# Moving the long inputs' norm, the order of the FFN combinations and the first gate loads in a hybrid encoder kernel

## The chip, the cores and the metric

The kernel runs on one core of a Trainium2 chip. The metric is the device time of one execution in microseconds (us), as the median of several runs; lower is better. The engines are TensorE (PE: matmuls; PEld: its weight loads), VectorE (DVE), ScalarE (ACT), GpSimd (POOL) and SyncE (SP), which issues most of the DMA transfers.

## What is computed

The reference is a small transformer trunk of one layer. It runs twice with the same weights: on a long input of 1024 tokens and on a short one of 512. To each, 16 learned meta tokens are prepended.

```python
h = concat([meta, x])                                  # 1040 or 528 tokens, 1024 wide
n = rms_norm(h, g_mix)
qa, ka, va, qb, kb, vb = split(n @ w_in)               # 2304 columns: 18 tiles of 128
qa, ka = rotate(rms_norm(qa)), rotate(rms_norm(ka))    # group A: 8 heads, 2 key/value heads
oa = softmax(qa ka / 8) va
qb, kb = rotate(qb), rotate(kb)                        # group B: 4 heads, two softmax maps each
ob = rms_norm((softmax(..0) - lam * softmax(..1)) vb)
h = h + concat(oa, ob) @ w_out
n = rms_norm(h, g_ffn)
gate = depthwise_conv3(n @ w_gate) + conv_b            # along the tokens; 2816 = 22 tiles of 128
h = h + (gelu(gate) * (n @ w_up)) @ w_down
y = rms_norm(h, g_final)[16:]
```

All of it is float32. The kernel keeps that precision by splitting each operand into a rounded part "hi" and a remainder "lo": a product is three matmuls, hi*hi, hi*lo and lo*hi (`mm3`, lines 121 to 123). A split is a cast on ACT (line 114) and a subtraction on DVE or POOL (line 115).

## The kernel before

**Stages.** The long input is `s = 0`, the short one `s = 1`.

1. `projection` of the short input (line 197): weights come as column tiles of 128, each is loaded (`load_weight`), split and multiplied with the eight row blocks of the input, in two token chunks (256 and 272). Tiles are taken as a key or query tile of group A, then a value tile, five times; then eight key and query tiles of group B. So there are 18 tiles with two chunks each, 36 products of 24 matmuls.
2. `projection` of the long input, in three chunks (384, 384, 272), merged with the short input's `attention`.
3. The long input's `attention`, merged with everything that the short input still has to do (`mixer_out`, `conv_glu`; in the program `f1`).
4. `mixer_out_long` (line 640): the long input's product with w_out and the residual add, in three parts of its tokens (342, 344 and 340 columns; a part holds a slice of the first half of the tokens and the same slice of the second half), eight column tiles each.
5. `conv_glu_long` (line 956): gate and up products of the long input, two weight tiles at a time, as a Winograd scheme: seven half-size products in place of eight. It needs sums and differences of the four quarters of the activations (half the width by half the tokens), and of the weights' quarters.
6. The down products in the same scheme, the last norm and the output.

**The projection's passes and norm.** Before its products the projection reads the input in eight row blocks (line 228), scales and splits each (lines 234 and 235) and squares it (line 238). For the long input POOL adds the squares into `acc` (line 245). Line 249 is the first product, of key tile KA, which needs no norm yet. Then, chunk by chunk, a matmul with a matrix of 1/1024 sums `acc` over the partitions (line 255), and `rsqrt_newton` (lines 98 to 108: Ln, Exp and Square on ACT, two passes on DVE) makes `rstd`; line 257 scales it. Line 312 multiplies a product by `rstd`. The long input's products and norm share a tag of two PSUM buffers, "mm"; the short one's use "s" (three) and "t" (two).

**The combinations.** `combine` (line 654) is a generator that works on a finished part of `mixer_out_long`: its norm (a matmul, line 657, into an "s" buffer, and `rsqrt_newton`), then eight scalings of `h` (line 667), then the sums and differences for the Winograd scheme: `minus` is a subtraction on DVE (line 680), `kept` a split into one of the tiles `XS`. These tiles lie where the short input's pools were, so they can be written only when its output has left. The steps of part p's generator (`late`) are taken during part p+1, two after each tile from the third on (`ML` = 2); what is left is drained at that part's end, and the last part's steps are taken within the first gate products, three after each. In each part and tile the product is added to the residual on DVE (line 728), which frees its "s" buffer and one of two `res` buffers; POOL then issues the store of `h` (line 729).

**The first gate products.** For the first pair of gate tiles the Winograd sums of the weights are made ahead and kept in DRAM (`presplit`, `g.wg`). The products of that pair are done in two chunks of columns, 342 and 170, since the last part's 170 columns come later. `product` in `winograd` (line 916) loads its operand pair (hi and lo, 256 KB each) in each chunk anew: 7 products x 2 chunks x 2, 28 loads on SP (line 923), into `w_hi` and `w_lo` tiles with five buffers each (`HB`). `load_gate` (line 968) loads the raw gate weights and computes the gate of the meta token: 16 small products on ACT (line 977), two reductions on DVE (line 979), two matmuls (line 1004). In the before, its loads for the first pair stand behind the 18th of those loads.

**What sets the order.** Instructions are written as a program of generators; `merge` takes turns between two of them by their progress. The order in each engine's queue is then written at build time by a planner: it simulates the kernel with durations of its own and, whenever an engine is free in that simulation, gives it the ready instruction that comes first in the program. So an instruction that is late in the program can be hoisted into a hole, and a high place in the program is only a preference. On the chip the queues are fixed and strictly in order. `behind(g, ins)` (line 75) adds one rule: what is written in its block and runs on the engine of `ins` is queued after `ins`. It adds no semaphore.

Of the kernel before, what the change touches and what calls it, by code (L numbers as in the profile page):

```python
# [1 line left out]

# [10 lines left out]
F32 = mybir.dt.float32  # L13
F32R = mybir.dt.float32r
# [6 lines left out]
P = 128  # L21
# [175 lines left out]
def projection(ctx, g, s, side, tag, tag2):  # L197
# [10 lines left out]
    rstd = xp.tile([P, n], F32, name="rstd")  # L208
    products = []

    def load_tables(which):
# [9 lines left out]
    with tc.tile_pool(name=f"ps{s}", bufs=2, side=side, reuse_waits="tile") as sp:  # L221
# [25 lines left out]
        first_ps = g.psum.tile(P, cw, tag)  # L247
        with behind(g, *g.short_products):
            products.append(dense(g, first_ps, first, xhi, xlo, c0, cw))
# [7 lines left out]
        scaled = nc.vector.tensor_scalar(out=rstd, in0=rstd, scalar1=-0.5, scalar2=None, op0=ALU.mult)  # L257
        g.norm_of_short = [last, scaled.ins]
    es = ExitStack()
    bp = pool(ctx, g, f"pb{s}", 2, side)  # L260
# [107 lines left out]
    for i in range(4):  # L368
        for j in (KB + i, QB + i):
            w = load_weight(g, wp, g.w_in[j], ahead=1 + s, lo_engine=nc.gpsimd if s == 0 else None)  # L370
            for c0, cw in chunks:
# [5 lines left out]
                yield 24 * cw  # L377
    if s == 1:

        g.short_products = products[13:14]  # L380

# [258 lines left out]
def mixer_out_long(ctx, g, wp, x, begin):  # L640
# [7 lines left out]
    hp = pool(ctx, g, "fh0", 2, "right")  # L648
    cm = max(2 * w + 2 * (o == 0) for o, w in PARTS)

    def halves(a, o, w):
# [48 lines left out]
    with ExitStack() as es:  # L700
        mp = pool(es, g, "fm0", 2, "right")
        for o, w in PARTS:
# [19 lines left out]
            for j in range(KT):  # L722
                wj = load_parts(g, wp, g.wo[j]) if j in PRE else load_halves(g, wp, g.w_out[j])
                rows = g.xT[0][j * P:(j + 1) * P]
                res = loaded("res", 2, rows[:, NMETA:], rows[:, NMETA - 1:NMETA])
                ps = g.psum.tile(P, cw, "s")
                dense(g, ps, wj, xhi, xlo, 0, cw, range(KT - 1, -1, -1))
                nc.vector.tensor_tensor(out=h[:, j], in0=ps, in1=res, op=ALU.add)
                nc.gpsimd.dma_start(out=halves(g.h[j], o, w),
                                    in_=h[:, j, :2 * w].rearrange("p (x t) -> p x t", x=2))  # L730
                if o == PARTS[-1][0] and j >= KT - 2:

                    sums.append(mp.tile([P, cm], F32, name="sq_p", tag="m", bufs=MB)[:, :cw])
                    nc.scalar.activation(sums[-1], h[:, j], AF.Square)
                else:
                    add_square(g, mp, acc, h, j, 0, cw, nc.gpsimd, 1)
                yield 24 * cw
                if late and j >= ML:
                    for _ in range(2):
                        next(late, None)  # L740
            if late:
# [155 lines left out]

def winograd(g, wp, up, x, raw, c0, cw, pre=None):

# [16 lines left out]
    def product(a, b, place):  # L916
        if pre is None:
            a = split_half(g, wp, a)
        else:
            i, half = place  # L920
            a = [wp.tile([P, H], F32R, name=nm, tag=nm, bufs=HB) for nm in ("w_hi", "w_lo")]
            for part, tl in enumerate(a):
                g.loads.append(nc.sync.dma_start(out=tl.bitcast(F32),
                                                 in_=pre[i, part, :, half * H:(half + 1) * H]).ins)
        ps = g.psum.tile(P, cw, "mm")
        for i in range(HT):
            mm3(g, ps, *block(a, i), b[0][:, i, c0:c0 + cw], b[1][:, i, c0:c0 + cw], i == 0, i == HT - 1)
        return ps
# [27 lines left out]
def conv_glu_long(ctx, g, wp, x, late, es_x, es_h):  # L956
# [8 lines left out]
    first = PARTS[-1][0]  # L965
    g.loads = []

    def load_gate(f0):


        with behind(g, *g.loads[17:18] if f0 == 0 else g.loads[-1:] if f0 == 2 else []):
            raw = [load_whole(wp, g, g.w_gate[f0 + i]) for i in range(2)]
# [10 lines left out]
    for f0 in range(0, NFF, 2):  # L983
# [4 lines left out]
        for c0, cw in ((0, first), (first, H - first)) if f0 == 0 else ((0, H),):  # L988
            for i, half, ps, rest in winograd(g, wp, up, x, raw if f0 else None, c0, cw, None if f0 else g.wg):
                t0 = 1 + half * H + c0  # L990
                nc.vector.tensor_tensor(out=gate[:, i, t0:t0 + cw], in0=ps, in1=rest, op=ALU.add)
                for _ in range(3):
                    next(late, None)
            if f0 + c0 == 0:
                drain(late)
        if f0 == 0:
            raw, first_sums = load_gate(f0)
        if not ap:
            es_h.close()
            ap = pool(es, g, "fa0", 1, "left")  # L1000
        act = ap.tile([P, 2, N], F32, name="act", tag="act", bufs=2)
        for i in range(2):
            ps = g.psum.tile(P, 2, "mm")
# [13 lines left out]
        if f0 + 2 == NFF:  # L1017
            with tc.issue_after(gelu.ins):
                nc.scalar.preload_act_table_set(EXP_LN)
        raw = [load_whole(up, g, g.w_up[f0 + i], "w_f2") for i in range(2)]  # L1020
        for i, half, ps, rest in winograd(g, wp, up, x, raw, 0, H):
            a = act[:, i, half * H:(half + 1) * H]
# [224 lines left out]
def drain(gen):  # L1247
    for _ in gen:
        pass


LAG = 5
NPRE = 4
# [17 lines left out]
def trunk_kernel(ctx, tc, g):  # L1271
# [69 lines left out]
    g.splits = []  # L1341
    with ExitStack() as es:
        drain(projection(es, g, 1, "right", "s", "t"))
    g.splits = None
    with ExitStack() as es0:
        p0 = projection(es0, g, 0, "left", "mm", "mm")
        with ExitStack() as es1:
            merge(attention(es1, g, 1, "right"), R1[0], p0, R1[1])
        drain(p0)
# [92 lines left out]
```

## Time and profile before

| | us |
|---|---|
| three runs | 2128.84, 2129.21, 2135.24 |
| their median | 2129.21 |
| the profiled execution | 2138.1 |
| its span, first to last instruction | 2136.3 |
| mean granted TensorE clock in it | 0.982 |
| PE busy | 2051.1 |
| DVE busy | 1724.1 |
| ACT busy | 1156.8 |
| POOL busy | 582.7 |

The profile is of one execution. Times in its rows count from the span's start. A row of the timeline is start, duration, engine, line, instruction, output<-inputs, shapes, how many in a row, and in brackets how long the engine sat idle before it and what ended that wait. PE's busy time is that of pipelined matmuls, whose shown durations overlap; the granted clock is 1.00 at full speed and 0.50 at half. In this execution the short products run to 152, the long input's projection beside the short one's attention from there to about 510, the three parts of `mixer_out_long` from 1320 to 1449, the gate and up products from there to 1900.

### The profile page before, as it was taken

Reading aid. Unit: us, or ns where it says so; the run is one execution under the profiler, and the core shown is the slowest. Engines: PE = TensorE matmul, PEld = TensorE weight load, DVE = VectorE, ACT = ScalarE, POOL = GpSimd, SP = SyncE. Lnnn points to the kernel's source line nnn. Section 1 sums busy time; section 2 is a strip of 40 time slices with the busy share of each in tenths; the row PEclk is TensorE's granted clock in tenths of the full one; section 3 lists DMA queues with packets and bytes.
Section 4 is the critical chain, followed back from the end, with each engine's and each line's share of the span. In section 5 each row is a group of like instructions: output and inputs, shape, how many; then the busy total and the mean of one; then the engine's idle time right before and its main releaser. Section 6 shows DMA issues by size and latency. Waiting matters only on the chain.

```text
span 2136.3 us, 35264 instructions
## 1 busy us (share of the span) xinstructions
PE 2051.1 (96%) x12302; PEld 1833.1 (86%) x12302; DVE 1724.1 (81%) x3786; ACT 1156.8 (54%) x2253; POOL 582.7 (27%) x534
## 2 busy tenths in 40 slices
PE   6999999999999999999999999979999999999998
PEld 6988888997887999899989999978888777778877
DVE  6878889767879788888988885578878878869886
ACT  6635566544657556666666765345444444435454
POOL 4653233553112000000000000542444444330112
PEclk8999999999999999999999999998999999999999
DMA  7564335456621322223352224986232232247443
GB/s 252 178 198 133 118 110 170 153 182 226 206 84 55 105 75 70 70 85 114 103 188 77 93 88 145 300 256 229 101 109 89 97 115 84 94 166 258 119 126 126
DMA packets 164897, 296.30 MB, mean 139 GB/s; under 512 B 21456, under 2 KB 82672, under 8 KB 164208
## 3 DMA queue, kind: packets, MB, share of 16 engines
q1 hardware_dynamic: 162416, 287.76, 41.6%
q0 software_dynamic: 2304, 6.29, 0.8%
q8 instruction: 97, 1.59, 0.3%
q14 instruction: 80, 0.66, 0.1%
HBM read 211.13 MB, written 82.85 MB: 138 GB/s over the span
## 4 chain that ended last, share of the span: by engine, by line
PE 76%; DVE 12%; DMA 4%; ACT 3%; issue 3%; POOL 1%; SPq 1%; DVEq 0%; ACTq 0%; POOLq 0%
PE ps_mm L121 17%; PE ps_mm L123 17%; PE ps_mm L122 17%; PE ps_t L456 5%; PE ps_s L431 3%; PE ps_s L432 3%; PE ps_s L121 2%; PE ps_s L122 2%; PE ps_s L123 2%; PE ps_o L471 2%; PE ps_o L470 2%; DVE p L433 1%; DVE w_lo L115 1%; DMA m<-oT 1%; DVE acc L979 1%
## 5 line engine op out<-in xcount | busy, mean ns | idle before, releaser
L121 PE MATMUL ps_mm<-xhi,w_hi 128*128 128x258 f32 (+3 forms) x1264 | 383.4, 304 | 12.0 <-ACT xhi L114 3.7
L122 PE MATMUL ps_mm<-xlo,w_hi 128*128 128x258 f32 (+3 forms) x1264 | 379.0, 300 | 0.3 <-POOL xlo L115 0.3
L123 PE MATMUL ps_mm<-xhi,w_lo 128*128 128x258 f32 (+3 forms) x1264 | 377.2, 299 | 0.3 <-DVE w_lo L115 0.3
L433 DVE TENSOR_SCALAR_CACHE_REDUCE p<-ps_s 114x344 f32<-114x344 f32 (+4 forms) x562 | 257.6, 488 | 30.2 <-PE ps_s L432 19.1
L114 ACT CAST pt_hi<-ps_t 128x512 fp32r<-128x512 f32 (+6 forms) x360 | 169.3, 483 | 181.0 <-PE ps_t L456 155.2
L121 PEld LDWEIGHTS ps_mm<-xhi,w_hi 128*128 128x128 f32 x1264 | 240.0, 190 | 17.5 <-ACT xhi L114 5.4
L438 ACT ACTIVATE p<-p,nm 114x1040 f32<-114x1040 f32 (+5 forms) x212 | 214.8, 1013 | 72.8 <-DVE nm L436 71.8
L115 DVE TENSOR_TENSOR w_lo<-w_f,w_hi 128x1024 fp32r<-128x1024 f32 (+1 forms) x182 | 192.8, 1067 | 66.2 <-ACT w_hi L114 65.6
L122 PEld LDWEIGHTS ps_mm<-xlo,w_hi 128*128 128x128 f32 x1264 | 240.3, 190 | 1.9 <-POOL xlo L115 0.7
L123 PEld LDWEIGHTS ps_mm<-xhi,w_lo 128*128 128x128 f32 x1264 | 240.0, 190 | 1.2 <-DVE w_lo L115 0.5
L114 ACT CAST w_hi<-w_f 128x1024 fp32r<-128x1024 f32 (+1 forms) x199 | 167.6, 856 | 84.9 <-PE ps_mm L122 57.5
L115 DVE TENSOR_TENSOR pt_lo<-ps_t,pt_hi 128x512 fp32r<-128x512 f32 (+4 forms) x312 | 171.7, 561 | 43.7 <-ACT pt_hi L114 42.3
L115 POOL TENSOR_TENSOR a_lo<-gate,a_hi 128x256 fp32r<-128x256 f32 x44 | 43.3, 985 | 545.3 <-ACT a_hi L114 525.9
L431 PE MATMUL ps_s<-k,q 128*114 128x348 f32 (+4 forms) x552 | 183.6, 338 | 3.4 <-DVE p L433 3.2
L456 PE MATMUL ps_t<-ident,p 128*128 128x128 f32 (+7 forms) x1188 | 183.0, 270 | 1.0 <-DVE nm L436 0.5
L432 PE MATMUL ps_s<-k,q 128*114 128x348 f32 (+4 forms) x552 | 171.1, 315 | 0.0
L121 PE MATMUL ps_s<-xhi,w_hi 128*128 128x256 f32 (+4 forms) x480 | 148.7, 313 | 20.4 <-ACT xhi L234 8.2
L456 PEld LDWEIGHTS ps_t<-ident,p 128*128 128x128 f32 (+7 forms) x1188 | 140.4, 136 | 29.6 <-issue 6.8
L123 PE MATMUL ps_s<-xhi,w_lo 128*128 128x256 f32 (+4 forms) x480 | 147.4, 307 | 1.4 <-DMA w_lo<-wo 1.4
L122 PE MATMUL ps_s<-xlo,w_hi 128*128 128x256 f32 (+4 forms) x480 | 148.6, 310 | 0.0
L121 PE MATMUL ps_mm<-t_hi,w_hi 128*128 128x512 f32 (+2 forms) x368 | 144.6, 393 | 1.2 <-DVE v L934 1.2
L123 PE MATMUL ps_mm<-t_hi,w_lo 128*128 128x512 f32 (+2 forms) x368 | 144.4, 392 | 0.1
(275 smaller groups left out, 5309.4 us busy)
## 6 DMA issues: line engine op xcount, KB each, us to landing
w_f<-w_gate SPq DMA_DIRECT2D x46, 512.0 KB, 3.5
w_f<-w_up SPq DMA_DIRECT2D x44, 512.0 KB, 3.4
w_f<-w_in SPq DMA_DIRECT2D x36, 512.0 KB, 3.9
a_f<-act SPq DMA_DIRECT2D x62, 256.0 KB, 2.7
w_f<-w_down SPq DMA_DIRECT2D x22, 512.0 KB, 3.3
act<-a_t SPq DMA_DIRECT2D x44, 256.0 KB, 2.1
a<-w_down SPq DMA_DIRECT2D x40, 256.0 KB, 5.4
w_hi<-wo SPq DMA_DIRECT2D x36, 256.0 KB, 5.1
```

Of the source, the lines that this page charges most:

```text
L114: return (nc.scalar.copy(hi, src).ins, (lo_engine or nc.vector).tensor_tensor(out=lo, in0=src, in1=hi.bitcast(F32), op=ALU.subtract).ins)
L115: (lo_engine or nc.vector).tensor_tensor(out=lo, in0=src, in1=hi.bitcast(F32), op=ALU.subtract).ins)
L121: nc.tensor.matmul(ps, lhsT=whi, rhs=xhi, start=start, stop=False)
L122: nc.tensor.matmul(ps, lhsT=whi, rhs=xlo, start=False, stop=False)
L123: return nc.tensor.matmul(ps, lhsT=wlo, rhs=xhi, start=False, stop=stop).ins
L431: nc.tensor.matmul(ps, lhsT=q[0], rhs=k[:, c0:c0 + cw], start=True, stop=False)
L432: nc.tensor.matmul(ps, lhsT=q[1], rhs=k[:, c0:c0 + cw], start=False, stop=True)
L433: nc.vector.tensor_scalar(out=p[:, c0:c0 + cw], in0=ps, scalar1=HD ** -0.5, scalar2=-3.0e38, op0=ALU.mult, op1=ALU.max, accum_out=mx[:, i: ...
L438: g.last_exp = nc.scalar.activation(p, p, AF.Exp, bias=nm, accum_out=l).ins
L456: nc.tensor.transpose(tps[:, c:c + M], p[:, k0:k0 + kw], g.ident[:M, :M])
L470: nc.tensor.matmul(o, lhsT=v[:, i, :], rhs=hi, start=i == 0, stop=False)
L471: nc.tensor.matmul(o, lhsT=v[:, i, :], rhs=lo, start=False, stop=False)
```

## The change

It has four parts.

- **Projection.** `projection` of the long input yields once when its passes, first product and norm are written. The short projection's generator is run for 24 chunks (`TN`), that is 12 of its 18 tiles; then the long one's first stretch is written; then the short one's last six tiles. Everything else of the long projection still follows after these. The first long product stays behind the 14th short one.
- **Combinations.** The two steps after each tile stand behind that tile's residual add on DVE.
- **First gate operands.** An operand pair is loaded in the first chunk and kept for the second. Five pairs stay in the five buffers of `w_hi` and `w_lo`; the other two go to a third tile `h` from the pool of `mixer_out_long` (two buffers), which is free when part 1's combinations are done. The raw gate weights' loads stand behind the last of the 14 loads that are left.
- **Meta token's sums.** For the first pair, the first two up products come ahead of the two matmuls of line 1004. For every pair the loads of the up weights are written before the gate's activation.

```diff
 def projection(ctx, g, s, side, tag, tag2):
+    if s == 1:
+        g.short_products = products
...
-        with behind(g, *g.short_products):
+        with behind(g, *(g.short_products[13:14] if s == 0 else [])):
             products.append(dense(g, first_ps, first, xhi, xlo, c0, cw))
...
         g.norm_of_short = [last, scaled.ins]
+    if s == 0:
+        yield 0
...
-    if s == 1:
-        g.short_products = products[13:14]

 def mixer_out_long(ctx, g, wp, x, begin):
     hp = pool(ctx, g, "fh0", 2, "right")
+    g.spare_h = lambda: hp.tile([P, KT, cm], F32, name="h", tag="h")
...
-                nc.vector.tensor_tensor(out=h[:, j], in0=ps, in1=res, op=ALU.add)
+                added = nc.vector.tensor_tensor(out=h[:, j], in0=ps, in1=res, op=ALU.add).ins
...
                 if late and j >= ML:
-                    for _ in range(2):
-                        next(late, None)
+                    with behind(g, added):
+                        for _ in range(2):
+                            next(late, None)

 def winograd(g, wp, up, x, raw, c0, cw, pre=None, kept=None, more=None):
...
+        elif place in kept:
+            a = kept[place]
         else:
             i, half = place
-            a = [wp.tile([P, H], F32R, name=nm, tag=nm, bufs=HB) for nm in ("w_hi", "w_lo")]
+            if len(kept) < HB:
+                a = [wp.tile([P, H], F32R, name=nm, tag=nm, bufs=HB) for nm in ("w_hi", "w_lo")]
+            else:
+                a = [more[:, (2 * (len(kept) - HB) + part) * H:][:, :H].bitcast(F32R) for part in range(2)]
+            kept[place] = a
             for part, tl in enumerate(a):
                 g.loads.append(nc.sync.dma_start(...))

 def conv_glu_long(ctx, g, wp, x, late, es_x, es_h):
+    more = g.spare_h().rearrange("p k c -> p (k c)")
     def load_gate(f0):
-        with behind(g, *g.loads[17:18] if f0 == 0 else g.loads[-1:] if f0 == 2 else []):
+        with behind(g, *g.loads[-1:] if f0 == 0 else g.loads[-1:] if f0 == 2 else []):
...
         act = ap.tile([P, 2, N], F32, name="act", tag="act", bufs=2)
+        raw = [load_whole(up, g, g.w_up[f0 + i], "w_f2") for i in range(2)]
+        products = winograd(g, wp, up, x, raw, 0, H)
+        ahead = [next(products)] if f0 == 0 else []
         for i in range(2):
             ps = g.psum.tile(P, 2, "mm")
             nc.tensor.matmul(ps, lhsT=first_sums[i], rhs=g.ones_d[:, 0:2], start=True, stop=True)
...
-        raw = [load_whole(up, g, g.w_up[f0 + i], "w_f2") for i in range(2)]
-        for i, half, ps, rest in winograd(g, wp, up, x, raw, 0, H):
+        for i, half, ps, rest in chain(ahead, products):

+TN = 24
 def trunk_kernel(ctx, tc, g):
...
-    with ExitStack() as es:
-        drain(projection(es, g, 1, "right", "s", "t"))
-    g.splits = None
     with ExitStack() as es0:
         p0 = projection(es0, g, 0, "left", "mm", "mm")
+        with ExitStack() as es:
+            p1 = projection(es, g, 1, "right", "s", "t")
+            for _ in range(TN):
+                next(p1)
+            next(p0)
+            drain(p1)
+        g.splits = None
         with ExitStack() as es1:
             merge(attention(es1, g, 1, "right"), R1[0], p0, R1[1])
```

More of the change, by code (lines that the diff above doesn't have):

```diff
@@ L1 @@
 from contextlib import ExitStack, nullcontext
+from itertools import chain
 import numpy as np
@@ L895, in presplit, with winograd @@
     yield 0
-def winograd(g, wp, up, x, raw, c0, cw, pre=None):
+def winograd(g, wp, up, x, raw, c0, cw, pre=None, kept=None, more=None):
     nc = g.nc
@@ L965, in conv_glu_long @@
     first = PARTS[-1][0]
-    g.loads = []
+    g.loads, kept = [], {}
+    more = g.spare_h().rearrange("p k c -> p (k c)")
     def load_gate(f0):
-        with behind(g, *g.loads[17:18] if f0 == 0 else g.loads[-1:] if f0 == 2 else []):
+        with behind(g, *g.loads[-1:] if f0 == 0 else g.loads[-1:] if f0 == 2 else []):
             raw = [load_whole(wp, g, g.w_gate[f0 + i]) for i in range(2)]
@@ L988, in conv_glu_long @@
         for c0, cw in ((0, first), (first, H - first)) if f0 == 0 else ((0, H),):
-            for i, half, ps, rest in winograd(g, wp, up, x, raw if f0 else None, c0, cw, None if f0 else g.wg):
+            for i, half, ps, rest in winograd(g, wp, up, x, raw if f0 else None, c0, cw, None if f0 else g.wg, kept, more):
                 t0 = 1 + half * H + c0
```

## The prediction

> **What bounds the kernel now.** I read the page first, for the busiest engine.
>
> ```profile
> span 2136.3 us, 35264 instructions
> ...
> PE 2051.1 (96%) x12302; PEld 1833.1 (86%) x12302; DVE 1724.1 (81%) x3786; ACT 1156.8 (54%) x2253; POOL 582.7 (27%) x534
> ```
>
> TensorE (PE) sets the time: 96% busy. An order that changes no amount of work can only win back PE's idle time, 2136.3 - 2051.1 = 85.2 us, and the time in which PE runs at half clock. So I asked next for PE's waits, longest first (who waited for whom: us in total, times, longest). The longest of all, and a short one, belong to lines that the change touches; two more stand below, under part A:
>
> ```profile
> PE ps_s L657 <- DVE h L728: 8.5, 1, 8.5
> ...
> PE ps_mm L121 <- DVE v L934: 1.2, 1, 1.2
> ```
>
> Then the busy table of the stretches around these waits. Its columns are the stretch, its length, each engine's busy time (and instructions), the granted clock, the DMA share and GB/s.
>
> ```profile
> 152.00:156.40 4.40, 1.70 (x7) 0.68 (x6) 2.87 (x5) 2.00 (x4) 2.24 (x3) 1.00 0.62 193
> 156.40:163.20 6.80, 4.74 (x15) 4.75 (x16) 2.20 (x4) 1.87 (x4) 0.55 (x3) 0.50 0.90 277
> ...
> 1390.00:1402.00 12.00, 11.58 (x70) 10.95 (x70) 7.57 (x13) 3.72 (x9) 7.39 (x10) 1.00 0.95 305
> 1402.00:1416.00 14.00, 11.23 (x64) 9.71 (x62) 8.05 (x16) 6.75 (x14) 7.95 (x13) 1.00 0.83 276
> 1416.00:1424.50 8.50, 0.04 (x1) 0.07 (x1) 8.26 (x12) 3.19 (x5) 0.00 (x0) 0.70 0.67 215
> 1424.50:1429.60 5.10, 5.10 (x16) 4.63 (x17) 2.70 (x4) 2.66 (x6) 3.96 (x5) 0.50 0.66 192
> 1429.60:1449.00 19.40, 18.39 (x115) 17.56 (x113) 18.28 (x27) 8.56 (x14) 6.64 (x8) 1.00 0.86 254
> 1449.00:1462.60 13.60, 13.60 (x86) 13.51 (x85) 11.47 (x17) 5.16 (x9) 4.28 (x2) 1.00 0.96 332
> 1462.60:1465.20 2.60, 2.60 (x26) 2.60 (x24) 2.60 (x5) 0.61 (x2) 0.00 (x0) 1.00 0.96 336
> 1465.20:1467.20 2.00, 0.70 (x6) 0.42 (x4) 2.00 (x4) 1.56 (x4) 0.00 (x0) 0.99 1.05 399
> 1467.20:1477.50 10.30, 10.30 (x48) 10.30 (x49) 8.03 (x13) 6.64 (x21) 0.00 (x0) 0.50 0.84 289
> 1477.50:1484.20 6.70, 6.70 (x20) 5.44 (x19) 6.60 (x10) 4.97 (x14) 1.28 (x1) 0.50 0.00 1
> ...
> 1500.00:1900.00 400.00, 396.70 (x1709) 318.08 (x1708) 330.40 (x377) 178.45 (x355) 179.98 (x118) 1.00 0.28 98
> ```
>
> Three places are to be seen: after the short projection (152 to 163), before the long inputs' second norm (1402 to 1430) and in the first gate products (1465 to 1484). Each has an idle PE and, after it, half clock. From 1500 to 1900 PE is idle for 3.3 of 400 us; nothing is to be had there.
>
> **Part A, the long inputs' passes and norm.** The moved step issues 9 loads on SP, the split of one weight, 16 ACT passes, 8 DVE passes, 21 POOL adds, 24 matmuls, and then three norm chunks: a matmul, three ACT and two DVE instructions each, one scaling on DVE. In program order they now pass the last six short tiles, that is six weight loads with their splits, twelve products, and the rotations' stores on SP. But the order is a planner's, and it had already hoisted all but the last two norm chunks:
>
> ```profile
> L245 POOL TENSOR_TENSOR acc<-acc,x x21: 941/1177/2012, 36.7 to 79.1; 128x384 f32<-128x384 f32 x14, 128x272 f32<-128x272 f32 x7
> ```
>
> The adds, which need the loads and the passes, were over by 81 us. So this part of the move costs and brings nothing: the cover is that PE has short products from 108 to 152. What really moves, in the timeline:
>
> ```profile
> 83.88 0.81 PE L255 MATMUL ps_mm<-acc,ones_d 128*128 128x384 f32 x2
> ...
> 152.19 0.81 PE L255 MATMUL ps_mm<-acc,ones_d 128*128 128x384 f32 x2
> ...
> 155.52 0.70 PE L255 MATMUL ps_mm<-acc,ones_d 128*128 128x272 f32 x2 [2.52 <-DVE rstd L106]
> ...
> 158.46 0.69 PE L121 MATMUL ps_mm<-xhi,w_hi 128*128 128x384 f32 x1 [2.24 <-DVE rstd L106]
> 158.91 0.70 DVE L257 TENSOR_SCALAR rstd<-rstd 128x1040 f32<-128x1040 f32 x1
> ...
> 159.95 0.18 POOL L504 CAST halo<-q 128x2 fp32r<-128x2 f32 x1 [4.02 <-DMA q<-qk]
> ```
>
> One of the two "mm" buffers holds the first product, so the norm chunks take turns in the other: matmul, Ln, Exp, Square, DVE, next matmul. The first went at 84, the other two only when the short tiles were out. In front of the last six tiles they lie beside those tiles' matmuls, and PE goes from the short products straight to the long ones. Won: 2.52 + 2.24, and half of the 4.74 us that PE worked at clock 0.50, 2.4: in all 7.2. What is late next is the attention's operand q, at 159.95 as before; until then PE has the second and third key products (158.46 less 152.19 is 6.3 us that they come earlier). Between nothing (the waits move along) and 7.2, I take 7.2, since the three rows carry it directly.
>
> Here the Trainium skill speaks against me. Its page "TensorE: Matmul & The Clock Gate", section "What's actually happening", has the clock drop after an idle window of about 3.4 us. No single wait between 152 and 163 is that long, nor is PE's pause at 1465, yet the stretches behind both show 0.50, so the trace disagrees and decides. By the page the 2.4 would not be this step's to win, and the sum would be 4.8 for A.
>
> **Part B, combinations behind adds.** The edges bind only DVE: in part p+1, the combination steps of part p stand behind the add of tile 2, 3 and so on. The chain of waits (start, us, what) and DVE's timeline (start, us taken, instruction) show what stands there now:
>
> ```profile
> 1388.92 1.45 DVE h L667 x3
> 1390.37 0.44 DVE h L728
> 1390.83 3.38 DMA res<-xT
> 1394.30 0.53 DVE h L728
> 1394.84 5.96 DMA res<-xT
> 1400.87 7.51 DMA m<-oT
> ```
> ```profile
> 1386.75 3.63 DVE L667 SCALAR_TENSOR_TENSOR h<-h,gain,rstd 128x340 f32<-128x340 f32 x6
> 1390.30 0.50 DVE L728 TENSOR_TENSOR h<-ps_s,res 128x344 f32<-128x344 f32 x1
> ...
> 1414.75 1.63 DVE L115 TENSOR_TENSOR x_lo<-h,x_hi 128x680 fp32r<-128x680 f32 x2
> ...
> 1423.80 0.93 DVE L728 TENSOR_TENSOR h<-ps_s,res 128x340 f32<-128x340 f32 x2
> ```
>
> Six L667, 3.63 us, stood ahead of the add at 1390.30; with edges two may stand there, 1.2 us. So the add, the residual loads behind it (two buffers, each free only after an add) and all later SP loads come 2.4 us earlier: queued behind the add are also POOL's store of h and the sum of squares. The 8.5 us wait is another matter: the adds at 1423.80 belong to part 2, the burst from 1414.75 to part 0, which stays ahead of part 2 in program order. No edge touches it; it moves only as far as its start does, and it starts once the short inputs' output lets go of its memory. Bounds: above, PE's losses (8.5 idle, 14.00 - 11.23 = 2.8, half of 5.10 = 2.5), 13.8, but DVE must do the same work before the gate and is idle from 1402 on for 14.00 - 8.05 + 8.50 - 8.26 + 5.10 - 2.70 + 19.40 - 18.28 + 13.60 - 11.47 = 11.8 us; below, 0, since the DMA share of 0.95 may eat an earlier issue. I take 3, near the 2.4 that the row shows. What the edges hold back in part 2 (its last step, three passes of 0.8 as in the burst) falls into a wait that DVE has anyway, for the third norm:
>
> ```profile
> 1451.03 0.57 DVE L106 SCALAR_TENSOR_TENSOR rstd<-ps_s,eps,rstd 128x340 f32<-128x340 f32 x1 [3.07 <-ACT rstd L105]
> ```
>
> Without that cover it would cost 2.5. The edges are an order in DVE's own queue and add no semaphore; behind a held combination wait ACT's casts of it and, last, the gate's products.
>
> **Part C, gate operands once, sums later.** The fourteen loads of this row (from the DMA issues of 1438 to 1470; count, KB each, median us to landing) and their fourteen w_lo twins become seven each; that is 14 x 256 KB less on DMA engines that are full here (share 0.96 to 1.05). Behind it stand a row of the chain of waits and one of DVE's timeline:
>
> ```profile
> w_hi<-wg SPq DMA_DIRECT2D x14, 256.0 KB, 5.1
> ```
> ```profile
> 1459.26 7.87 DMA w_lo<-wg
> ```
> ```profile
> 1466.09 0.50 DVE L934 TENSOR_TENSOR v<-ps_mm,u 128x342 f32<-128x342 f32 x1
> ```
>
> The load issued at 1459.26 landed at 1467.13, where PE's third 170-wide matmul waited for it. But PE's 1.2 us wait before that is for L934, which frees PSUM at 1466.59: that wait takes the place of the loads'. Won: 1467.13 - 1466.59 = 0.5. Two operand pairs now go to a spare h tile, so SP waits for part 1's last combination; w_up, w_gate and w_down loads are queued behind. The pair is needed by the sixth of seven products, about 1449 + 5/7 of 13.6 = 1458.7; issued by 1451, when DVE's last held pass is through, and 5.1 under way, it lands at 1456. Cost taken: 0 (0 to 2, if it is a long one such as the 7.87). The sums' products and reductions only move behind two 512-wide products and lie under them: 0. The up weights' loads of later groups come earlier on SP: 0, PE has no gap there.
>
> The half clock after 1467.2 costs (49 weight loads in 10.30, against 24 in 2.60: 10.30 - 49 x 0.108 = 5.0) plus half of 6.70, 8.3 in all. I credit none of it, because it may not be in the timed runs: the profiled execution took 2138.1, 8.9 above their median of 2129.21.
>
> **Sum.** 7.2 + 3 + 0.5 = 10.7. Against the profiled execution's 2138.1 that gives 2127.4; against the median, **2118.5**. The forecast's own range is 2112 to 2123.
>
> **Rivals.**
>
> *All three places open* (chance 0.18). The short inputs' output ends earlier, the burst spreads over DVE's idle 11.8, the clock stays up: 7.2 + 8 to 11.8 + 0.5, and up to 8.3: 2113 down to 2101. For it: DVE idles 5.9 us just before the burst. Against: DVE is full from 1462.6 to 1467.2.
>
> *The clock after the norm isn't bought back* (0.08): the two waits go and PE still runs at 0.50 for a stretch there, since DMA-bound starts of the attention leave it thin. 2118.5 + 2.4 = 2120.9. By the clock gate page of the Trainium skill this is the case to expect.
>
> *The norm's waits move* (0.18). PE takes its queue in order; if the planner puts the second and third L255 too close together among the short tiles, the 2.52 and 2.24 appear there. Then only 3.5 are left: 2125.7, no change.
>
> *DVE becomes the bound at the gate: slower* (0.16). With fewer loads ahead of them the raw gate weights land earlier, and their sums move up into the stretch where DVE is full:
>
> ```profile
> 1469.75 1.91 DVE L979 TENSOR_REDUCE acc<-prod 128x128 f32<-128x1024 f32 x1
> ```
>
> ```profile
> L977 ACT ACTIVATE prod<-w_f,x 128x128 f32<-128x128 f32 x16 | 4.9, 387 | 2.2 <-DVE acc L979 2.2
> ```
>
> Two reductions ahead of L934 hold PSUM 3.8 us longer; one weight's eight products on ACT, in front of the t_hi cast that DVE waits for, 8 x 0.387 = 3.1 more; and so long a wait makes the half clock certain, 8.3 that the timed runs may not pay now. With B lost in the same queue: 2129.2 - 7.2 - 0.5 + 15.2 = 2136.7. It decides once a reduction stands ahead of the second L934. Against it: the sums are later in program order, so they come first only where the planner sees DVE idle.
>
> **How the numbers follow.** The forecast has 0.40. A run of this kernel can be told from no change at about 0.3%, 6.4 us, so faster means below 2122.8 and slower above 2135.6. Faster: 0.38 of the forecast, 0.06 of the clock case, 0.18 of the first rival: 0.62. Same: 0.04 of these two, 0.15 of the moved waits, 0.04 of the last: 0.23. Slower: 0.15. The range goes from within the first rival, 2103, to the last one's price, 2137.
>
> **What would show it.** A: L255's three chunks before the last short product, no L106 wait of PE, granted clock 1.00 at 156. B: at most two L667 between the adds of part 1, a first add of part 2 still behind x_lo/t_lo passes, PE's wait at L657 near 6 us. C: 14 loads of wg, a wait for L934 of about a microsecond left. I am wrong if L657's wait is gone or grown, or if L979 stands ahead of L934.

## The result, and the profile after

The changed kernel is slower: 2144.36 us (median of four runs) against 2130.77, a ratio of 1.0063 (95% interval 1.0049 to 1.0077), that is 13 us (10 to 16). I had forecast 2118.5 and a range up to 2137. The profiled execution after took 2142.1 (span 2140.3). That it lies only 4.0 us above the one before is due to the one before: of 35 further runs of the kernel before only one, at 2137.66, came near its 2138.1, and their median is 2129.27.

Line numbers after are up to 14 higher: 116 is the lo pass (115 before), 434 a score matmul (431), 661 the norm of a part (657), 671 the scaling (667), 732 the residual add (728), 946 and 1005 the gate's additions (934, 991), 993 the meta sums' reduction (979). In the experiments they lie a few lines off these; the names of the tiles tell which is meant.

The page after, and TensorE's waits of that kernel:

```profile
span 2140.3 us, 35241 instructions
...
PE 2049.3 (96%) x12302; PEld 1832.2 (86%) x12302; DVE 1737.8 (81%) x3786; ACT 1156.5 (54%) x2253; POOL 580.8 (27%) x534
```
```profile
PE ps_s L661 <- DVE h L732: 8.5, 1, 8.5
...
PE ps_s L434 <- DVE p L436: 5.6, 5, 2.2
...
PE ps_mm L123 <- DVE t_lo L116: 3.9, 2, 3.6
```

No wait for the norm is left. Idle PE is 2140.3 - 2049.3 = 91.0 us, 5.8 more than before. Where it is, the busy table after shows (columns as in the prediction):

```profile
152.00:156.40 4.40, 4.39 (x24) 3.78 (x23) 1.21 (x3) 0.76 (x2) 1.54 (x2) 1.00 0.72 212
156.40:163.20 6.80, 5.43 (x36) 4.72 (x35) 3.00 (x9) 3.53 (x7) 1.21 (x4) 1.00 0.91 281
...
200.00:300.00 100.00, 96.11 (x595) 86.69 (x593) 82.88 (x245) 58.76 (x131) 28.42 (x28) 0.97 0.39 118
300.00:400.00 100.00, 92.71 (x577) 85.47 (x576) 89.84 (x284) 60.66 (x158) 35.55 (x25) 0.91 0.47 145
...
1471.00:1488.10 17.10, 13.72 (x54) 12.85 (x55) 10.28 (x20) 8.57 (x17) 3.86 (x3) 0.50 0.21 72
```

and the same two stretches before:

```profile
200.00:300.00 100.00, 97.09 (x616) 87.62 (x617) 84.48 (x250) 59.97 (x135) 30.77 (x29) 1.00 0.41 125
300.00:400.00 100.00, 94.63 (x621) 86.70 (x621) 86.82 (x293) 64.05 (x167) 35.21 (x25) 1.00 0.49 151
```

At 152 to 163 all is as forecast: PE busy 9.82 of 11.20 us in place of 6.44, at clock 1.00. Between 200 and 400, which my sum left alone, PE is busy 2.9 us less and the granted clock falls to 0.97 and 0.91. And at the gate stands the rival that I had given 0.16. VectorE's timeline, then TensorE's waits there:

```profile
1464.12 0.51 DVE L1005 TENSOR_TENSOR gate<-ps_mm,u 128x342 f32<-128x342 f32 x1
1464.55 1.98 DVE L993 TENSOR_REDUCE acc<-prod 128x128 f32<-128x1024 f32 x1
1466.44 1.64 DVE L116 TENSOR_TENSOR t_lo<-h,t_hi 128x680 fp32r<-128x680 f32 x2
1467.99 0.51 DVE L946 TENSOR_TENSOR u<-ps_mm,u 128x342 f32<-128x342 f32 x1
...
1469.61 1.90 DVE L993 TENSOR_REDUCE acc<-prod 128x128 f32<-128x1024 f32 x1
...
1473.46 0.86 DVE L116 TENSOR_TENSOR t_lo<-h,t_hi 128x680 fp32r<-128x680 f32 x1
```
```profile
1470.12 0.46 PE L122 MATMUL ps_mm<-t_hi,w_hi 128*128 128x170 f32 x2 [1.31 <-ACT t_hi L115]
...
1474.38 0.51 PE L123 MATMUL ps_mm<-t_lo,w_hi 128*128 128x170 f32 x1 [3.58 <-DVE t_lo L116]
```

One reduction stands ahead of the first 342-wide L946, the other ahead of the last t_lo passes, and PE waits for t_hi and t_lo. Half clock follows for 17.1 us, as long as it does in the trace of before (10.30 and 6.70 in the prediction's table).

### The profile page after: what moved, and what is told of

Same layout as the page of the kernel before. It is cut to its first block, busy times and chain, and to the rows that moved or that the text cites. A ratio compares the mean times of both kernels' runs of the same rounds, so it can differ in the third digit from the quotient of the medians.

```text
span 2140.3 us, 35241 instructions
## 1 busy us (share of the span) xinstructions
PE 2049.3 (96%) x12302; PEld 1832.2 (86%) x12302; DVE 1737.8 (81%) x3786; ACT 1156.5 (54%) x2253; POOL 580.8 (27%) x534
## 4 chain that ended last, share of the span: by engine, by line
PE 75%; DVE 13%; DMA 4%; issue 3%; ACT 3%; POOL 1%; SPq 1%; DVEq 0%; ACTq 0%; POOLq 0%
PE ps_mm L122 17%; PE ps_mm L124 17%; PE ps_mm L123 17%; PE ps_t L459 5%; PE ps_s L434 3%; PE ps_s L435 3%; PE ps_s L123 2%; PE ps_s L122 2%; PE ps_s L124 2%; DVE w_lo L116 2%; PE ps_o L474 2%; PE ps_o L473 1%; DVE p L436 1%; DVE acc L993 1%; DMA m<-oT 1%
## 5 line engine op out<-in xcount | busy, mean ns | idle before, releaser
L436 DVE TENSOR_SCALAR_CACHE_REDUCE p<-ps_s 114x344 f32<-114x344 f32 (+4 forms) x562 | 257.8, 488 | 28.4 <-PE ps_s L435 15.2
L123 PE MATMUL ps_mm<-t_lo,w_hi 128*128 128x512 f32 (+2 forms) x360 | 141.6, 393 | 3.9 <-DVE t_lo L116 3.9
```

The source lines that it names most:

```text
L123: nc.tensor.matmul(ps, lhsT=whi, rhs=xlo, start=False, stop=False)
L436: nc.vector.tensor_scalar(out=p[:, c0:c0 + cw], in0=ps, scalar1=HD ** -0.5, scalar2=-3.0e38, op0=ALU.mult, op1=ALU.max, accum_out=mx[:, i: ...
```

## The experiments

In each, the time is compared with runs of the kernel before that stand beside it; a ratio of 1.001 is 2.1 us. The ratio is an estimate from all of these runs and not the quotient of the two medians; `a_r08` and `a_held_fill` have five runs, the others eleven or twelve.

### Each part alone

`a_alone` has the projection's part of the diff, `b_alone` the two hunks of edges, `cd_alone` the gate's two parts, `d_alone` only the later sums:

```diff
+        raw = [load_whole(up, g, g.w_up[f0 + i], "w_f2") for i in range(2)]
+        products = winograd(g, wp, up, x, raw, 0, H)
+        ahead = [next(products)] if f0 == 0 else []
         for i in range(2):
             ps = g.psum.tile(P, 2, "mm")
...
-        for i, half, ps, rest in winograd(g, wp, up, x, raw, 0, H):
+        for i, half, ps, rest in chain(ahead, products):
```

> Only the long inputs' passes and norm stand in front of the last six short tiles; the combinations, the gate operands and the meta sums are as before. Theory 1 (the projection and the attention of the short inputs lose more than the early norm wins): 4 to 8 us slower than before, ahead of it by about 7 us at 160 us and behind it by 2 to 5 us at 540 us. Theory 2 (what the changed kernel loses sits at the gate, and the trace of before was an unlucky one there): 3 to 7 us faster than before, and the 2.5 and 2.2 us waits for the norm are gone without new ones.

> Only the edges: the steps of a combination stand behind the add of the tile before them. My prediction: 3 us faster (0 to 5), at most two passes of h<-h,gain,rstd between two adds of part 1, and PE's longest wait (for the first add of part 2) unchanged but for its start, 8 us. Rival (the edges push the last passes of part 1 and with them those of part 2 towards the gate's products): 2 to 5 us slower, lost between 1440 and 1480 us.

> Only the gate: operands of the first gate products loaded once, meta sums' products behind the first up product; edges and norm as before. Theory 1 (the raw gate weights now land earlier, and two reductions of 1.9 us stand on VectorE in front of the t_lo passes that TensorE waits for): 3 to 5 us slower, all of it between 1465 and 1480 us, with a wait of 3 us or more for t_lo. Theory 2 (the gate is neutral, as predicted; the wait for t_lo comes from the edges): within 1.5 us of before.

> Only the order at the end of the gate: the meta sums' products (and what needs them) stand behind the first up product; the gate operands are loaded twice as before, no edges, norm as before. Theory 1 (the loads are what moves the reductions up; the later sums by themselves only take away TensorE's wait for the second sum, 3.1 us in the kernel with the edges alone): 1 to 4 us faster than before, no wait of TensorE for acc. Theory 2 (the later sums cost, since up weights then pass the gate's): 2 us or more slower.

| | median | before | ratio (95%) | us |
|---|---|---|---|---|
| a_alone | 2134.92 | 2129.27 | 1.0031 (1.0020 to 1.0042) | +6.6 |
| b_alone | 2130.26 | 2129.27 | 1.0008 (0.9994 to 1.0022) | +1.7 |
| cd_alone | 2135.46 | 2129.27 | 1.0037 (1.0025 to 1.0048) | +7.9 |
| d_alone | 2129.62 | 2128.51 | 1.0001 (0.9992 to 1.0011) | +0.2 |

(The last column is the ratio less one, times 2129.) The three parts add up to 16.2, near the 13.4 of the whole. Two lose; the edges and the later sums do nothing that can be measured. The gate operands were not run without the later sums, so that the 7.9 is theirs follows from `cd_alone` against `d_alone`. Theory 1 holds for the norm. For the gate it holds in kind only: 7.9 us where 3 to 5 were expected, and TensorE waits more for t_hi (3.93) than for t_lo (1.15). For the later sums neither expectation came.

My 3 us for the edges were not there. In `b_alone` the add of part 1 came 1.5 us after the first scaling (1377.40 and 1375.88), where it had come 3.6 us after it (1390.30 and 1386.75): 2.0 us earlier, for the 2.4 of the forecast. But the DMA share is 0.98 there, and in the 12 us from 1380 PE, waiting for weights, is busy for 10.46, no more than the 11.58 of before. The busy table of `b_alone`:

```profile
1365.00:1380.00 15.00, 15.00 (x98) 14.57 (x96) 13.40 (x21) 5.81 (x14) 12.59 (x19) 1.00 0.98 315
1380.00:1392.00 12.00, 10.46 (x64) 9.71 (x63) 7.62 (x13) 3.75 (x10) 6.54 (x8) 1.00 0.84 286
```

The kernel `b_alone` runs the stages up to 1330 exactly as before, so it serves as a second trace of before there. The busy table of `b_alone`, then of `a_alone`:

```profile
140.00:160.00 20.00, 15.23 (x107) 14.22 (x106) 11.86 (x22) 6.88 (x14) 9.18 (x14) 0.92 0.54 176
160.00:200.00 40.00, 36.81 (x215) 33.78 (x215) 32.94 (x109) 19.97 (x47) 13.50 (x19) 0.87 0.39 130
...
200.00:500.00 300.00, 292.27 (x1907) 274.48 (x1906) 234.25 (x699) 165.96 (x403) 120.67 (x102) 0.99 0.46 147
```
```profile
140.00:160.00 20.00, 19.99 (x149) 19.38 (x148) 10.29 (x21) 5.47 (x11) 10.04 (x13) 1.00 0.50 163
160.00:200.00 40.00, 35.55 (x216) 32.37 (x215) 36.03 (x110) 20.27 (x46) 16.38 (x21) 0.96 0.50 169
...
200.00:500.00 300.00, 285.56 (x1848) 268.28 (x1847) 239.75 (x693) 163.45 (x397) 117.94 (x100) 0.98 0.43 140
```

To 200 the early norm wins 3.5 us of idle PE (60 - 52.04 against 60 - 55.54) and up to 5.2 us of clock (0.08 of 20 and 0.09 of 40). From 200 to 500 it loses 6.7 us of busy PE, and some 3 us by the clock (0.98 of 300 us in place of 0.99). The gain is real, and more than all of it goes in a stage that the edit does not touch.

These two sums leave 1 us of loss, and the runs show 6.6. Counting the columns that TensorE has worked off (128x384 is 384), `a_alone` is 8.1 us ahead of `b_alone` at 200, 3.1 behind at 500, 5.4 at 545 and 8.9 at 1300. The part behind 500 can't be put down to the edit: the kernel before, in the order of `b_alone` to there, is 8.9 us behind `b_alone` at 1300 too.

### Where the norm stands, and the mix behind it

`a_alone` with one constant changed:

```diff
-TN = 24
+TN = 30                                   # a_tn30
...
-R1, R2, R3 = (1.0, 0.9), (1.0, 0.4), (1.0, 20.0)
+R1, R2, R3 = (1.0, 0.8), (1.0, 0.4), (1.0, 20.0)   # a_r08
```

> The early norm alone, in front of the last three short tiles and not the last six. Theory 1 (the loss after 200 us comes from the first long products, which start 6 us earlier against the attention, wherever the norm stands): 4 to 9 us slower than before, as with six tiles, with the same waits between 300 and 400 us. Theory 2 (each place of the norm gives another plan of the attention's stage, better or worse by chance): another set of waits there, and a time that differs from that with six tiles by more than 3 us.

> The early norm alone (in front of the last six short tiles), and the long projection's share beside the short attention lowered from 0.9 to 0.8, so that the attention runs ahead again. Theory 1 (the early long products put the projection ahead of the attention and so work on VectorE together at 300 to 400 us): the waits between 300 and 400 us fall from 9.2 to 5 us or less, and the kernel is 4 us or more faster than with the early norm alone. Theory 2 (any other mix loses against the one of before): as slow as the early norm alone or slower, 6 us or more above before.

`a_tn30` 2134.76 against 2128.51, ratio 1.0028 (1.0018 to 1.0038); `a_r08` 2138.01, 1.0040 (1.0027 to 1.0052). So the place of the norm does not matter (theory 1), and a smaller share of the long projection does not help: my first guess at the mechanism, too much projection over the whole stage, falls. In both, the third chunk of long products still runs ahead of the attention's first scores (from 158 and 156 us).

### That one chunk held back

```diff
     def product(w, c0, cw):
         ps = g.psum.tile(P, cw, tag)
-        products.append(dense(g, ps, w, xhi, xlo, c0, cw))
+        with behind(g, *(g.scores[5:6] if s == 0 and len(products) == 2 else [])):
+            products.append(dense(g, ps, w, xhi, xlo, c0, cw))
```

(`g.scores` collects the second matmul of each score product. The chunk is the third of the key tile KA, and it is queued behind the sixth score product.)

> The early norm alone, with one order added on TensorE: the long projection's third chunk product stands behind the first six score matmuls of the short attention, as it does in the kernel before (with the early norm it ran ahead of them). Theory 1 (that one chunk of lead is what makes another order of the 200 to 500 us, with its waits and half clock): the waits between 200 and 500 us fall back from 14.4 us to 8, and the kernel is 1 to 5 us faster than before (TensorE then waits 2 to 4 us for q at 157 us). Theory 2 (the early norm itself costs there, by other passes on VectorE): still 4 us or more slower than before.

2123.64 against 2128.31: ratio 0.9980 (0.9968 to 0.9991), 4 us faster than before and 11 faster than `a_alone`. TensorE now waits for q, and the later waits are those of before again. The timeline and the waits (160 to 400 us) of `a_held`, then the waits of `b_alone` and of `a_alone`, and a row of the busy table of `a_held`:

```profile
159.11 1.00 PE L434 MATMUL ps_s<-k,q 128*128 128x264 f32 x3 [3.58 <-DMA q<-qk]
```
```profile
PE ps_mm L121 <- DVE hn L106: 2.1, 1, 2.1
PE ps_o L474 <- DVE pt_lo L115: 1.4, 2, 0.8
PE ps_s L434 <- DVE p L436: 1.3, 3, 0.5
```
```profile
PE ps_mm L339 <- DVE t L333: 3.3, 2, 2.3
PE ps_mm L121 <- DVE hn L106: 2.1, 1, 2.1
PE ps_o L471 <- DVE pt_lo L115: 1.5, 2, 0.9
PE ps_s L431 <- DVE p L433: 1.2, 3, 0.5
```
```profile
PE ps_s L433 <- DVE p L435: 5.2, 4, 2.2
PE ps_mm L121 <- DVE t L317: 2.2, 1, 2.2
```
```profile
200.00:500.00 300.00, 291.05 (x1900) 273.37 (x1899) 232.77 (x695) 162.50 (x395) 123.29 (x107) 0.99 0.47 150
```

TensorE's idle time from 200 to 500 is 9.0 us, 7.7 in `b_alone` and 14.4 in `a_alone`. An idle of 3.6 us in front of the attention is cheaper than the 24 matmuls that filled it: with them ahead, the planner wrote another order for all that follows. The traces show that order: of the 754 groups of like instructions that VectorE runs in `b_alone` from 162 to 500, 725 stand in the same sequence in `a_held` and 502 in `a_alone` (TensorE: 1593 and 1282 of 1621).

### The meta sums held back

```diff
-            for k in range(KT):
-                nc.scalar.activation(prod[:, k], ...)
-            nc.vector.tensor_reduce(out=acc, ...)
+            with behind(g, *g.adds[3:4] if f0 == 0 else []):
+                for k in range(KT):
+                    nc.scalar.activation(prod[:, k], ...)
+                nc.vector.tensor_reduce(out=acc, ...)
```

(`g.adds` collects the gate's additions; the fourth is the last 342 wide.) `sums_held` has it on the changed kernel, `cd_held` on `cd_alone`.

> The changed kernel, but the first pair's meta sums (ScalarE's products and VectorE's reductions) are held behind the last of the four 342-wide gate additions. Theory 1 (the two reductions of 1.9 us in front of t_lo cost the wait of 3.6 us and make the stretch at half clock there): 4 to 8 us faster than the changed kernel, so 6 to 10 us slower than before, no wait for t_lo over 1 us. Theory 2 (VectorE is full there whatever the order; its burst of 680-wide passes is what is late): within 1.5 us of the changed kernel, 12 to 15 us slower than before.

> The gate part alone (operands once, later sums), without edges and early norm, with the first pair's sums held behind the last of the four 342-wide gate additions. Theory 1 (the 7.9 us that the gate part lost are the reductions and ScalarE's products ahead of the t passes): 6 to 9 us faster than the gate part alone, so from 2 us faster to 2 us slower than before; no wait for t_hi or t_lo over 2 us. Theory 2 (they are the fewer, earlier loads themselves): still 5 us or more slower than before.

`sums_held`: 2134.98 against 2129.27, 1.0030 (1.0018 to 1.0043), so 7 us of the 13 come back. `cd_held`: 2128.36 against 2128.51, 0.9995 (0.9986 to 1.0005), all of the 7.9. Theory 1 holds in both, but for its sign that no wait for t_lo over 1 us is left in `sums_held` (1.7). The rule binds only what runs on the engine of the addition, VectorE, so it holds the two reductions; ScalarE's products come later only where they wait for a reduction (the first eight still run at 1452.20 in `cd_held`). What had put the sums there is the loads, which `cd_held` issues nearly as early (1445.40) without the loss. The SP queue's issues of the first two pairs of raw gate weights, before and in `cd_alone`:

```profile
1457.77 0.90 SPq L150 DMA_DIRECT2D w_f<-w_gate  x2
...
1469.34 5.16 SPq L150 DMA_DIRECT2D w_f<-w_gate  x2
```
```profile
1442.87 1.44 SPq L151 DMA_DIRECT2D w_f<-w_gate  x2
...
1452.20 4.99 SPq L151 DMA_DIRECT2D w_f<-w_gate  x2
```

Of the 14.9 and 17.1 us between these times, 7.6 are that `cd_alone` came there earlier as a whole (its last norm stands at 1440.92, before at 1448.53); the rest is the gate part's, which has 14 loads in front of them in place of 18 and more. ScalarE's timeline in `cd_alone`, then TensorE's waits in `cd_alone` and in `cd_held`:

```profile
1461.47 2.45 ACT L988 ACTIVATE prod<-w_f,x 128x128 f32<-128x128 f32 x8 [3.98 <-DVE acc L990]
1463.82 1.41 ACT L115 CAST t_hi<-h 128x680 fp32r<-128x680 f32 x2
```

```profile
1464.62 0.51 PE L122 MATMUL ps_mm<-t_hi,w_hi 128*128 128x170 f32 x1 [3.93 <-ACT t_hi L115]
1466.27 0.51 PE L123 MATMUL ps_mm<-t_lo,w_hi 128*128 128x170 f32 x1 [1.15 <-DVE t_lo L116]
```
```profile
1462.69 0.34 PE L122 MATMUL ps_mm<-t_hi,w_hi 128*128 128x170 f32 x1 [0.28 <-ACT t_hi L115]
1464.30 0.35 PE L123 MATMUL ps_mm<-t_lo,w_hi 128*128 128x170 f32 x1 [1.26 <-DVE t_lo L116]
```

The eight products at 1461.47 are already the second pair's. They had waited for the second reduction to free the one `prod` buffer, and the casts of t_hi stand behind them.

### The price of the half clock

(`g.last_dense` is the last product of `mixer_out_long` so far; nothing reads `fill`.)

```diff
+        if o == PARTS[1][0]:
+            fill = g.psum.tile(P, P, "o")
+            with behind(g, g.last_dense):
+                for _ in range(34):
+                    nc.tensor.matmul(fill, lhsT=g.ones_d, rhs=g.ones_d, start=True, stop=True)
         ps = g.psum.tile(P, cw, "s")
```

> The kernel before with 34 matmuls of ones by ones (128 wide, 7.5 us at full clock, nothing reads them) in the 8.5 us wait ahead of the norm in the middle of the long mixer output; nothing else differs. Theory 1 (a wait makes half clock when it leaves TensorE idle for 2 us or more of one window of 3.41 us, and that half clock costs as much as a short wait): no half clock after the wait, where all traces so far have 10.2 us of it, so 5 us faster. Theory 2 (the half clock there comes from something else, such as the DMA-fed products behind the wait): within 1.5 us of before.

> The gate part alone with its sums held, and the same 34 matmuls in the wait. If the two are independent: 5 to 6 us faster than before (1 us of the held sums, 5 us of the clock).

`fill` 2125.52 against 2128.31, 0.9990 (0.9977 to 1.0002); `cd_held_fill` 2128.09, 0.9990 (0.9976 to 1.0005). Neither can be told from no change, and neither reaches the 5 us that I had expected; in `cd_held_fill` the two medians differ by 0.2 us only. TensorE's timeline of `fill`, two stretches behind the wait in `fill`, and the stretch before that is like the first:

```profile
1406.76 7.75 PE L659 MATMUL ps_o<-ones_d 128*128 128x128 f32 x68
1415.41 0.82 PE L662 MATMUL ps_s<-acc,ones_d 128*128 128x344 f32 x2 [0.91 <-DVE h L733]
...
1438.24 0.84 PE L662 MATMUL ps_s<-sq_p,ones_d 128*128 128x340 f32 x2 [1.97 <-ACT sq_p L739]
```
```profile
1414.50:1425.00 10.50, 9.60 (x61) 9.42 (x61) 8.19 (x16) 4.59 (x9) 4.19 (x6) 1.00 0.74 205
...
1436.00:1444.00 8.00, 6.03 (x26) 5.57 (x26) 4.82 (x10) 2.40 (x6) 0.68 (x1) 0.79 1.00 357
```
```profile
1424.50:1435.00 10.50, 10.50 (x51) 10.03 (x52) 8.06 (x15) 4.75 (x9) 4.59 (x6) 0.76 0.71 193
```

Each of the 34 runs in two passes, hence 68. The clock stays at 1.00, where it was 0.76 on the mean, as theory 1 says. Of the 5 us that I had put on it, 1.0 goes into the next wait: for the squares of the last part TensorE waited 1.01 us before and waits 1.97 now. Behind that wait comes half clock that was not there before (0.79 over 8 us, about 1.7). By these rows some 2.4 would be left, near the 2 of the runs.

### Put together

`all_held_fill` is the changed kernel without the edges, with both orders and the 34 matmuls; `mended` the whole changed kernel with both orders; `a_held_fill` is `a_held` with the 34 matmuls.

> Early norm with the third chunk held, gate part with its sums held, and the 34 matmuls in the wait; no edges. If theory 1 holds for each: 7 to 11 us faster than before, the fastest kernel of all. If the early norm costs by itself: slower than the same kernel without it.

> The whole changed kernel, edges included, with the two orders put back: the long projection's third chunk behind the first six score matmuls, and the first pair's meta sums behind the last 342-wide gate addition. Theory 1 (these two orders are all that the change lost): 13.4 us of loss less what the two give back alone (6.6 + 4.7 = 11.3 for the chunk, 7.9 + 1.1 = 9 for the sums) is 7 us faster than before; anything from 2 to 8 us faster agrees. Theory 2 (the parts together lose something that none loses alone): no faster than before.

> The early norm with the third chunk held, and the 34 matmuls of ones in the 8.5 us wait; gate and edges as before. If the gains of the two add: 6 to 8 us faster than before (4.7 and 2 to 3). If the wait for the squares and the first gate products takes back what the clock gives, as the trace of the 34 matmuls alone suggests: 4 to 5 us faster, as without them.

| | median | before | ratio (95%) |
|---|---|---|---|
| all_held_fill | 2125.16 | 2128.31 | 0.9984 (0.9974 to 0.9994) |
| mended | 2125.28 | 2127.92 | 0.9990 (0.9979 to 1.0001) |
| a_held_fill | 2121.90 | 2127.92 | 0.9965 (0.9953 to 0.9978) |

`mended` settles where the loss came from: with just two orders back, the whole change goes from 13 us slower to 2 faster, and the interval just reaches no change. It lies at the lower end of what I had expected; neither the gate part nor the edges bring anything of their own that can be measured. `all_held_fill` missed its 7 to 11: 3.4 us, where the ratios of its parts alone add up to 7.5 (4.3, 2.1 and 1.1), and why is open. The best version is `a_held_fill`, about 7 us faster than before, without gate part and edges; there the gains do add.

## Why the prediction was wrong

**Part A, the gain: right.** The three chunks of the norm stood beside the short tiles, no wait for it was left, the clock was 1.00 at 156. In `a_alone` the place won 3.5 us of idle and up to 5.2 us of clock, for my 7.2. The signs that I had named for it all came, but all of them lay ahead of 163 us. The third rival (moved waits) did not come, and the second (the clock not bought back) only in part: the changed kernel still has one stretch at half clock there, 170.52 to 177.35, where before had 156.40 to 163.20 and one more from 183.8.

**Part A, the step that failed** is "What is late next is the attention's operand q, at 159.95 as before; until then PE has the second and third key products". I took the third product as cover for the wait for q, at no cost. It put a chunk of 24 matmuls in front of the attention's first scores, and the planner wrote a new order for the whole stage behind, with more waits for VectorE and about 10 us lost from 200 to 500. `a_held` shows it: with that chunk behind the first scores, 11 us return (6.6 + 4.3). I had costed the moved step and not the order of the stage that it leads into, though front and prediction both say that the order is a planner's.

**Part B, 3 us: wrong, the lower bound was right.** `b_alone` gives +1.7 (-1.3 to 4.7), so 0 is within it and 3 won is not. The failed step is "near the 2.4 that the row shows": the add came 2.0 earlier, and PE was no busier behind it. That the DMA engines, share 0.95 before and 0.98 in `b_alone`, ate the earlier issue is argued from these shares and not tested. That no edge touches the 8.5 us wait was right: it is 8.51 after. The sign "near 6 us" did not follow from that argument, and it did not come.

**Part C, 0.5: wrong, and the slow rival's mechanism is what came.** The failed step is "The sums' products and reductions only move behind two 512-wide products and lie under them: 0". The matmuls of the sums do; ScalarE's products and VectorE's reductions follow their loads, which came earlier, and went up into the full stretch. The rival named the place, the two reductions and ScalarE's products in front of t_hi; its price, 15.2, was too high by more than half against 1.7 + 7.9 = 9.6, and TensorE waited for t_hi and t_lo and not for PSUM that L934 holds. So the wait of a microsecond for L934, my sign for C, did not come; the 14 loads did. `cd_held` shows that the order is all of it (0.9995, so from 3.0 us faster than before to 1.1 slower). I gave this 0.16 with the argument that the sums are later in program order, which the early loads outweighed.

**The sum** missed by 25.9 us: the 10.7 that did not come, 13.6 that were lost, in a stage without a term and at a term of 0.5, and 1.6 by which the median of before lay higher beside the runs after. By parts, against their runs alone: A 13.8 (7.2 won, 6.6 lost), C 8.4 and B 4.7, together 26.9. No case of mine had a loss in both places, so the range ended at 2137.

What stays open: which of VectorE's passes makes the other order of 200 to 500 worse. That it is the order is shown by `a_held`; the passes were not moved one by one. Open too is where the part of the 6.6 us that is not lost by 500 goes.

## What to carry to other kernels

When an edit lets one engine start something earlier, ask what now stands ahead of what in the queues behind it, not only what the early start fills; where a planner writes the queues, one product more ahead can cost a whole stage, and a short wait can be the better buy. A load that lands earlier also pulls up everything that hangs on it: hold work that nobody needs yet behind the burst by an order of its own. Time the parts alone before believing the sum.

## What the runs showed of the hardware

The clock goes by a grid. In all sixteen traces each step of the granted clock lies on a grid of 3.413 us (off by 0.01 at most), whose start differs from execution to execution. I cut the traces at that grid and took TensorE's idle time in each window at full clock: of the windows with 2.0 us idle or more, 94 of 94 were followed by half clock, of those with 1.4 to 2.0 us 53 of 103, of those with 1.0 to 1.4 five of 130 (the drain at the end left out; each count shifts by up to four with how the grid is laid). It need not be one wait. In the busy table after, two waits of 0.93 and 1.38 us fall into one window, and with TensorE fully busy behind them two windows go at half clock:

```profile
317.20:320.70 3.50, 1.19 (x8) 0.70 (x7) 3.39 (x10) 2.16 (x7) 2.08 (x2) 1.00 0.00 0
320.70:327.50 6.80, 6.80 (x22) 6.04 (x23) 6.72 (x27) 4.04 (x10) 2.40 (x4) 0.50 0.46 164
```

The Trainium skill, page "TensorE: Matmul & The Clock Gate", section "What's actually happening", gives a free-running window of 3413 ns, and the traces agree; it has the clock drop after an idle window, and here a window idle for 2.0 of its 3.41 us was enough, so the measurement decides.

So a wait of about 2 us costs its own length and, by where it falls on the grid, nothing or half of 3.4 or 6.8 us more. That is probably why 35 runs of the kernel before spread from 2121.76 to 2137.66: the mean clock of the first is 0.987, of the last 0.980, and by my estimate 0.007 of 2130 is 14.9 of these 15.9 us. It is also why its one trace, with 17.1 us of half clock at the gate where `b_alone` has 3.4, was a poor sample.
